# A two-layer encoder on one core: stored-order window projections, 128-row splits, more square buffers and an interleaved last norm

## The chip, the core and the metric

The kernel runs on one core of one Trainium2 chip. TensorE (PE in the profile, with its weight loads as PEld), VectorE (DVE), ScalarE (ACT), GpSimd (POOL) and SyncE (SP), which issues nearly all DMAs, each work through a list of instructions in order and wait for each other through semaphores. The metric is the device time of one execution in microseconds (us). A time is the median of several runs.

## The reference

The kernel computes two layers over 1024 tokens of 1024 features, in fp32, and a last RMSNorm:

```
for l in range(2):
    h = rmsnorm(x, norm_gain[l])
    mk, mv = split(rmsnorm(mem) @ w_mem_kv[l])          # 256 memory tokens
    if l == 0:
        qa, ka, va, qb, kb, vb, qm, gate = split_cols(h @ w_in_even)
        ya = global_gqa(rope_2d(rmsnorm(qa)), rope_2d(rmsnorm(ka)), va)   # 8 heads, 2 kv heads
        yb = window_gqa(qb, kb, vb, sink, rel_bias)                       # 8 heads, +-128 tokens
        ym = memory_attn(qm, mk, mv)                                      # 4 heads of 128
        x = x + (concat(ya, yb, ym) * silu(gate)) @ w_out_even
    else:
        qc, kc, vc, qm, gate = split_cols(h @ w_in_odd)
        yc = neighborhood_attn(qc, kc, vc, rpb)                           # 16 heads, 8x16 window
        ym = memory_attn(qm, mk, mv)
        x = x + (concat(yc, ym) * silu(gate)) @ w_out_odd
return rmsnorm(x, final_norm_gain)
```

## The kernel before

Every fp32 operand of a matmul is held as two parts, a high part rounded for TensorE (`wh`, `ah`, `ph`, the high rows of `q`, `k`, `H`) and a low part, the difference (`wl`, `al`, `pl`). A product is three matmuls: high by high, high by low, low by high. So each weight tile that arrives by DMA (`wraw`) is split: a copy makes the high part, a subtraction the low one. `wsplit` names the engines for the two steps in each stage (lines 131 to 144). Activations lie as features on the 128 rows by tokens on the columns; a projection of 128 features over 1024 tokens is two halves of 24 matmuls of 128x512 (line 223), summed in a PSUM bank `pj`.

The program runs through these stages (times of the profiled execution):

- 0 to 165 us: memory tokens and inputs are loaded and normalised; `mem_keys` (line 489) and `mem_values` (line 518) project the memory for both layers and store keys and values in the DRAM buffer `kv`; the global heads' queries and keys are projected in units of 256 tokens by `a_unit` (line 767), normalised and rotated with the tokens on the rows (`rope`, lines 782 to 801), turned back by TensorE (`back`) and split (`k_unit`, `q_unit`, lines 834 and 849). One half of each tile's rows holds the high part, the other the low part, of one head.
- 165 to 500 us: global attention in pairs of heads (scores in lines 949 and 950, `pv` in line 982).
- 500 to 665 us: window attention in pairs of heads (scores in lines 627 and 628, transposes in line 120, `pv` in line 668). The projections `q_pair`, `k_pair`, `v_pair` for windows are evaluated in natural order of tokens. The tokens are stored in another order: 8 blocks of columns of the 16x64 grid, each with 16 rows of 8. Natural reading makes the moving operand a view of runs of eight floats (`tokens`, `natural=True`). What waits in `self.waiting` (steps of three matmuls of the gate projections, of query projections, of the first output products) is put between the parts of a window pair by `pull`.
- 665 to 790 us: `out_project` of layer 0 (line 1185); the residual sum in line 1194, the squares for the next norm in line 1199 (`square`), their sum on POOL in line 1201.
- 790 to 960 us: `front`, the projections of layer 1; 960 to 1400 us: layer 1's memory and neighbourhood attention.
- 1400 us to the end: `out_project` of layer 1 and the last norm in two halves of 256 tokens each: sums of squares by TensorE (line 264), reciprocal root, turned to rows (line 120), scaled and stored (lines 1619 to 1622).

The order on each engine is made by a scheduler that simulates the program: it moves instructions by priorities (`AHEAD`, `ahead`), by `issue_after` (not before a named matmul has been issued), and keeps the order that is pinned (`Pinned`) on an engine. So the order must be read from the built program.

## Time and profile before

| what | us |
|---|---|
| median of 3 runs (1526.03 to 1527.65) | 1527.34 |
| the profiled execution | 1526.59 |
| its span | 1524.8 |
| TensorE busy (PE) | 1483.9 |
| VectorE busy (DVE) | 1056.7 |
| ScalarE busy (ACT) | 838.3 |
| GpSimd busy (POOL) | 669.4 |
| mean granted clock of TensorE | 0.99 |

A row of a timeline has the start in us, the duration, the engine, the line, the operation, what it writes and reads, and in brackets how long its engine stood idle before it and what released it. A row of the waits has engine, line, releaser, then the sum of the waits, how many, and the longest. A row of a stretch has busy times of the engines, the granted clock (1.00 is full speed), the busy share of the DMA engines and GB/s. A group's row ends with busy time, mean ns of one, and the idle time before them. Times come from one profiled execution; its 1526.59 us lies 0.75 below the median.

### The profile page before, as it was taken

How to read it: one execution, taken by the hardware profiler on the slowest of the kernel's cores; microseconds unless marked ns; L12 is line 12 of the kernel's file. 1: busy time of each engine (PE TensorE's matmuls, PEld its weight loads, DVE VectorE, ACT ScalarE, POOL GpSimd, SP SyncE). 2: the span in 40 equal slices, each digit the busy share in tenths (PEclk: the TensorE clock that was granted, in tenths of full speed). 3: DMA queues.
4: the chain of work that ended last, by engine and by line, in shares of the span. 5: the costliest groups of instructions: out<-in, count | busy, mean ns of one | idle time of the engine just before them, and what ended most of it. 6: DMA issues, size and time to landing. Idle time of an engine off the chain costs nothing.

```text
span 1524.8 us, 25015 instructions
## 1 busy us (share of the span) xinstructions
PE 1483.9 (97%) x8217; PEld 1272.8 (83%) x8217; DVE 1056.7 (69%) x2292; ACT 838.3 (55%) x1854; POOL 669.4 (44%) x793
## 2 busy tenths in 40 slices
PE   8999999999999999999999999999999999999997
PEld 7898898989888788878878777877788888888886
DVE  6688777777676678876577865453477777777754
ACT  7754665555655455655444544453366666666543
POOL 1424546455554545443440000233356566664354
PEclk9999999999999999999999999999999999999998
DMA  8954324233232323287652434575555666678844
GB/s 289 280 166 132 118 70 138 84 101 105 99 99 96 112 67 111 99 287 249 198 183 78 145 116 154 201 243 172 177 167 183 186 205 205 205 218 290 303 120 136
DMA packets 165379, 250.91 MB, mean 165 GB/s; under 512 B 14465, under 2 KB 96641, under 8 KB 164225
## 3 DMA queue, kind: packets, MB, share of 16 engines
q1 hardware_dynamic: 164816, 249.22, 50.6%
q8 instruction: 65, 1.06, 0.3%
q14 instruction: 66, 0.53, 0.1%
q10 hardware_dynamic: 432, 0.09, 0.0%
HBM read 164.32 MB, written 74.45 MB: 157 GB/s over the span
## 4 chain that ended last, share of the span: by engine, by line
PE 85%; DVE 5%; DMA 4%; ACT 2%; issue 2%; POOL 1%; SPq 0%; DVEq 0%; ACTq 0%; POOLq 0%
PE pj L223 28%; PE tr L120 8%; PE pv L982 4%; PE x L1355 4%; PE pj L1185 4%; PE sa L1185 3%; PE pv L1021 3%; PE tr L1185 3%; PE s L1185 2%; PE y L1355 2%; PE pj L373 2%; PE pv L1355 2%; PE sa L949 2%; PE sa L950 2%; PE pv L1185 2%
## 5 line engine op out<-in xcount | busy, mean ns | idle before, releaser
L223 PE MATMUL pj<-H,wh 128*128 128x512 f32 x1280 | 424.9, 412 | 0.6 <-DVE vt L294 0.4
L223 PE MATMUL pj<-H,wl 128*128 128x512 f32 x640 | 252.9, 395 | 0.0
L112 ACT ACTIVATE ph<-tr 128x512 fp32r<-128x512 f32 (+2 forms) x336 | 180.5, 540 | 128.8 <-PE tr L120 123.4
L223 PEld LDWEIGHTS pj<-H,wh 128*128 128x128 f32 x1280 | 220.5, 189 | 33.8 <-PE sa L628 0.8
L470 DVE TENSOR_TENSOR pl<-tr,ph 128x512 fp32r<-128x512 f32 (+2 forms) x336 | 205.0, 615 | 50.6 <-ACT ph L112 48.6
L142 POOL TENSOR_SCALAR wh<-wraw 128x512 fp32r<-128x512 f32 x78 | 50.6, 649 | 279.5 <-DMA g<-P 160.7
L223 PEld LDWEIGHTS pj<-H,wl 128*128 128x128 f32 x640 | 120.4, 188 | 28.6
L112 ACT ACTIVATE wh<-wraw 128x384 fp32r<-128x384 f32 (+1 forms) x162 | 88.1, 552 | 93.5 <-PE pj L1185 11.8
L143 POOL TENSOR_TENSOR wl<-wraw,wh 128x512 fp32r<-128x512 f32 x86 | 113.3, 1318 | 24.7 <-ACT wh L112 20.6
L120 PE MATMUL tr<-ident,P 128*128 128x128 f32 x752 | 116.0, 273 | 2.0 <-POOL P L651 2.0
L1139 POOL TENSOR_TENSOR wl<-wraw,wh 128x384 fp32r<-128x384 f32 x56 | 61.0, 1090 | 107.3 <-ACT wh L112 97.3
L957 POOL TENSOR_SCALAR P<-P,st 128x1024 f32<-128x1024 f32 x64 | 75.7, 1184 | 65.5 <-DVE st L956 65.5
L1052 POOL TENSOR_SCALAR pn<-pn,st 128x384 f32<-128x384 f32 (+1 forms) x128 | 74.9, 588 | 66.8 <-DVE st L1051 37.4
L1050 ACT ACTIVATE pn<-pn,st 128x384 f32<-128x384 f32 (+1 forms) x128 | 75.1, 587 | 41.7 <-DVE st L1049 34.3
L120 PEld LDWEIGHTS tr<-ident,P 128*128 128x128 f32 x752 | 89.1, 140 | 10.5 <-POOL P L651 3.1
L955 ACT ACTIVATE P<-sa,st 128x1024 f32<-128x1024 f32 x64 | 71.6, 1119 | 45.1 <-DVE st L954 25.8
L954 DVE TENSOR_REDUCE st<-sa 128x1 f32<-128x1024 f32 x64 | 77.5, 1217 | 10.4 <-PE sa L950 9.2
L767 PE MATMUL pj<-ah,H 128*128 128x256 f32 x384 | 73.3, 289 | 3.3 <-DVE rqn L793 1.5
L1139 DVE TENSOR_TENSOR wl<-wraw,wh 128x384 fp32r<-128x384 f32 (+1 forms) x64 | 49.4, 771 | 28.5 <-ACT wh L112 28.4
L1046 DVE CUSTOM_DVE_ANT_0 pn<-s,bm 128x384 f32<-128x384 f32 x96 | 53.2, 555 | 19.8 <-PE tr L120 14.7
L982 PE MATMUL pv<-ph,va 128*128 128x256 f32 x256 | 66.6, 285 | 0.0
L982 PE MATMUL pv<-pl,va 128*128 128x256 f32 x256 | 65.8, 284 | 0.0
(488 smaller groups left out, 3919.8 us busy)
## 6 DMA issues: line engine op xcount, KB each, us to landing
wraw<-w_o SPq DMA_DIRECT2D x62, 256.0 KB, 3.5
y<-yb SPq DMA_DIRECT2D x24, 512.0 KB, 3.5
wraw<-s SPq DMA_DIRECT2D x64, 192.0 KB, 3.6
y<-sg SPq DMA_DIRECT2D x23, 512.0 KB, 3.5
wraw<-w_e SPq DMA_DIRECT2D x44, 256.0 KB, 3.0
k<-k SPq DMA_DIRECT2D x40, 256.0 KB, 4.3
wraw<-w_mem SPq DMA_DIRECT2D x32, 256.0 KB, 3.9
v<-v SPq DMA_DIRECT2D x8, 1024.0 KB, 4.8
```

The source lines that it names most:

```text
L112: return self.nc.scalar.activation(out, in_, AF.Copy, scale=scale)
L120: self.turned = self.fence = self.nc.tensor.transpose(o, i, self.ident)
L143: (nc.gpsimd if self.wsplit[1] == "pool" else nc.vector).tensor_tensor(lf, raw, hf, op=OP.subtract)
L223: nc.tensor.matmul(a[:, :n], s[:, kt % UNIT, :], m, start=(kt == 0 and i == 0), stop=(kt == KT - 1 and i == 2))
L470: nc.vector.tensor_tensor(pl[:, :n], tr[:, :n], ph[:, :n], op=OP.subtract)
L954: nc.vector.tensor_reduce(st[:, 0:1], s, axis=AX.X, op=OP.max, negate=True)
L957: self.normal = nc.gpsimd.tensor_scalar(pt, pt, st[:, 2:3], 0.5, op0=OP.mult, op1=OP.mult)
L982: nc.tensor.matmul(o[:, :256], v[:, c + k, kv, :], part[:, k * 256:(k + 1) * 256], start=(c + k == 0 and part is parts[0]), stop=(c + k == ...
L1050: nc.scalar.activation(o, o, AF.Exp, bias=st[:, 1:2], accum_out=st[:, 2:3])
L1139: engine.tensor_tensor(lf, raw, hf, op=OP.subtract)
L1185: last = nc.tensor.matmul(bank, s[:, k, :], y[3 * u + k][m][:, cols], start=start and u + k + e == 0, stop=u == 1 and k + e == 4, skip_gro ...
L1355: self.last = nc.tensor.matmul(bank, ws[s][:, k, :], b[k][m], start=start and k + i == 0, stop=k == UNIT - 1 and i == 2, skip_group_check= ...
```

## The change

Several edits come together:

1. `q_pair` and `k_pair` of the windows project in stored order; the sinks write the result into natural order (`columns`). `v_pair` stays.
2. `mem_values` of layer 0 splits its weights with `wsplit` "both": the low parts take turns on VectorE and POOL.
3. `mem_keys` splits 512 columns at once, `mem_values` uses two tiles of tag "so"; stores for keys are half as many.
4. `back` splits a turned tile on all 128 rows into a high and a low tile. `k_unit` and `q_unit` then place the halves by DMA: for the first query pair into the resident tiles `q0` and the DRAM buffer `qa`, for the second into `qa` alone; for the keys by six DMAs at the end, of which the last two read what they overwrite in the first.
5. `pull(10)` stands ahead of the last window pair.
6. `square` takes its tile from tag "ph" (three buffers in layer 0, four in layer 1) instead of "bt" (one).
7. `finish` replaces the last norm: difference, sum, root, rows and scaling of the two halves are interleaved in a pinned order on VectorE, the turned rows go to two banks, POOL scales three of eight tiles in each half.

```diff
-        (nc.gpsimd if self.wsplit[1] == "pool" else nc.vector).tensor_tensor(lf, raw, hf, op=OP.subtract)
+        e = self.either() if self.wsplit[1] == "both" else nc.gpsimd if self.wsplit[1] == "pool" else nc.vector
+        e.tensor_tensor(lf, raw, hf, op=OP.subtract)
...
+    def columns(self, t, c, n, natural):
+        if not natural:
+            return t[:, c:c + n]
+        return t.rearrange("p (r b c) -> p b r c", b=8, r=16)[:, c // 128:(c + n) // 128]
...
+            if natural:
+                vt = self.st("vt", [128, 512])
+                nc.vector.scalar_tensor_tensor(vt, p, 0.125, self.rows[:, c:c + n], op0=OP.mult, op1=OP.mult)
+                vt = vt.rearrange("p (b r c) -> p b r c", r=16, c=8)
+                self.copy(a[0:64], vt[0:64])
+                self.copy(b[64:128], vt[64:128])
+                nc.vector.tensor_tensor(a[64:128], vt[0:64], a[0:64], op=OP.subtract)
+                nc.vector.tensor_tensor(b[0:64], vt[64:128], b[64:128], op=OP.subtract)
+                return
...
-        self.tokens(w, nt, sink, natural)
+        self.tokens(w, nt, sink)
...
-                    for i in range(2):
-                        hl = [self.st(tag, [128, MEM], F32R) for _ in range(2)]
-                        self.split(*hl, vt[:, i * MEM:(i + 1) * MEM])
-                        for e, t in enumerate(hl):
-                            nc.sync.dma_start(dst[h + i, :, e, :], t.bitcast(F32))
+                    kk = [self.st(tag, [128, 512], F32R) for _ in range(2)]
+                    self.split(*kk, vt)
+                    for e, t in enumerate(kk):
+                        nc.sync.dma_start(dst[h:h + 2, :, e, :].rearrange("h p n -> p h n"),
+                                          t.bitcast(F32).rearrange("p (h n) -> p h n", h=2))
...
-    def back(self, rp, to):
+    def back(self, rp, h, l):
...
+        self.split(h, l, p)
...
+        def end():
+            self.back(rp, *(t[:, c] for t in ks[0]))
             if q == 3:
+                one, two = slice(0, 64), slice(64, 128)
+                for a, b in zip(*ks):
+                    for t, o, f, i in ((b, two, a, two), (b, one, a, two), (a, two, a, one)):
+                        nc.sync.dma_start(t[o].bitcast(F32), f[i].bitcast(F32))
...
+        def end():
+            hl = [self.st("so", [128, 512], F32R) for _ in range(2)]
+            self.back(rp, *hl)
+            for i in range(2):
+                s, o = slice(64 * i, 64 * i + 64), slice(64 - 64 * i, 128 - 64 * i)
+                for to, f in zip((s, o), hl):
+                    f = f[s].bitcast(F32).rearrange("p (t n) -> p t n", t=2)
+                    if pair == 0:
+                        nc.sync.dma_start(q0[i][to, c].bitcast(F32), f[:, 0])
+                        nc.sync.dma_start(qd[1][i, to, c], f[:, 1])
+                    else:
+                        nc.sync.dma_start(qd[0][pair:pair + 2, i, to, c].rearrange("t p n -> p t n"), f)
...
-        self.wsplit = ("act", "pool")
-        end.append(self.mem_values(w0, mem, kvd[0], "mv"))
+        self.wsplit = ("act", "both")
+        end.append(self.mem_values(w0, mem, kvd[0], "so"))
...
-            sq = self.st("bt" if k else "vt", [128, 512])
+            sq = self.st("ph" if k else "vt", [128, 512])
...
+        product(y, p, ws, True, cols[0])
+        difference(p, cols[0])
+        p = self.ps("pj")[:, :256]
+        end = product(y, p, ws, True, cols[1], range(3))
+        with tc.issue_after(end.ins):
+            sum_up(0, sums, True)
+            sum_up(0, [sq], False)
+        with tc.issue_after(self.last.ins):
+            end = product(y, p, ws, True, cols[1], range(3, 6))
+            sum_up(1, sums, True)
...
+                self.pull(10)
             self.window_pair(qb, kb[j // 2], vb, j // 2, 2 * j, sink, y, 1 if j == 2 else 2)
```

GpSimd's (POOL) list in the first stage, from the splits `wl` of the memory values' weights to the splits `al` of the first query weights; `rp` is the sum that ends a rotation. Before:

```order
L143 TENSOR_TENSOR wl_712<-wraw_709,wh_711 128x512
L143 TENSOR_TENSOR wl_724<-wraw_721,wh_723 128x512
L143 TENSOR_TENSOR wl_736<-wraw_733,wh_735 128x512
L143 TENSOR_TENSOR wl_748<-wraw_745,wh_747 128x512
L801 TENSOR_TENSOR rp_929<-rt_182_911,rt_187_925 128x256
L143 TENSOR_TENSOR wl_760<-wraw_757,wh_759 128x512
L753 TENSOR_TENSOR al_808<-wraw_805,ah_807 128x512
```

And now, on the same engine:

```order
L144 TENSOR_TENSOR wl_688<-wraw_685,wh_687 128x512
L144 TENSOR_TENSOR wl_712<-wraw_709,wh_711 128x512
L144 TENSOR_TENSOR wl_736<-wraw_733,wh_735 128x512
L818 TENSOR_TENSOR rp_919<-rt_181_901,rt_186_915 128x256
L144 TENSOR_TENSOR wl_760<-wraw_757,wh_759 128x512
L818 TENSOR_TENSOR rp_943<-rt_188_925,rt_193_939 128x256
L770 TENSOR_TENSOR al_808<-wraw_805,ah_807 128x512
```

Every other `wl` has left this list for VectorE; the first `rp` still stands ahead of the last `wl`.

VectorE's (DVE) list at the end of layer 0: `rows` adds the last square to the sum, `t` are low parts of weights for the next projections, `rq_v` begins the reciprocal root. Before:

```order
L1194 TENSOR_TENSOR yb_8084<-yb_8084,tr_8075 128x512
L1567 TENSOR_TENSOR rows_1675_8071<-vt_8889,bt_9203 128x512
L398 TENSOR_TENSOR t_1974_9362<-wraw_9366,t_1970_9358 128x512
L267 TENSOR_SCALAR rq_v_9316<-pv_9311 128x4
L398 TENSOR_TENSOR t_1975_9363<-wraw_9370,t_1971_9359 128x512
L237 TENSOR_SCALAR rq_i_9318<-rq_v_9316 128x4
L398 TENSOR_TENSOR t_1976_9364<-wraw_9374,t_1972_9360 128x512
L238 TENSOR_SCALAR rq_y_9319<-rq_i_9318 128x4
```

And now:

```order
L1207 TENSOR_TENSOR yb_8026<-yb_8026,tr_8017 128x512
L1656 TENSOR_TENSOR rows_1664_8013<-vt_8831,ph_9145 128x512
L415 TENSOR_TENSOR t_1963_9304<-wraw_9308,t_1959_9300 128x512
L415 TENSOR_TENSOR t_1964_9305<-wraw_9312,t_1960_9301 128x512
L415 TENSOR_TENSOR t_1965_9306<-wraw_9316,t_1961_9302 128x512
L268 TENSOR_SCALAR rq_v_9258<-pv_9253 128x4
L238 TENSOR_SCALAR rq_i_9260<-rq_v_9258 128x4
L239 TENSOR_SCALAR rq_y_9261<-rq_i_9260 128x4
```

The three splits `t` now stand together, ahead of the root.

TensorE's (PE) list at the end of the program; `pj` are the last products, `pv` the sums of squares, the rest turns the roots to rows. Before:

```order
L1185 MATMUL pj_17314<-H_17126,wh_17255 128x256 x2
L1185 MATMUL pj_17314<-H_17126,wl_17256 128x256
L264 MATMUL pv_17283<-inv_d_67,vt_16980 128x1
L264 MATMUL pv_17337<-inv_d_67,vt_16980 128x1 x2
L264 MATMUL pv_17283<-inv_d_67,bt_17259 128x1 x2
L264 MATMUL pv_17337<-inv_d_67,bt_17259 128x1 x2
L120 MATMUL tr_17297<-ident_63,iq_y_17290 128x128 x2
L120 MATMUL tr_17351<-ident_63,iq_y_17344 128x128 x2
```

And now:

```order
L1312 MATMUL pv_17205<-inv_d_67,vt_16922 128x1 x2
L1312 MATMUL pv_17205<-inv_d_67,ph_17204 128x1 x2
L1198 MATMUL pj_17228<-H_17066,wh_17197 128x256 x2
L1198 MATMUL pj_17228<-H_17066,wl_17198 128x256
L1198 MATMUL pj_17228<-H_17067,wh_17197 128x256 x2
L1198 MATMUL pj_17228<-H_17067,wl_17198 128x256
L1198 MATMUL pj_17228<-H_17068,wh_17197 128x256 x2
L1198 MATMUL pj_17228<-H_17068,wl_17198 128x256
L1312 MATMUL pv_17206<-inv_d_67,vt_16922 128x1 x2
L120 MATMUL tr_17264<-ident_63,rq_y_17255 128x128 x2
L120 MATMUL pj_17267<-ident_63,rq_y_17255 128x128 x2
L1312 MATMUL pv_17206<-inv_d_67,ph_17204 128x1 x2
```

The first half's sum has moved in between the second half's products; the second half's sum stands behind the first half's turning.

155 lines of the change are left out of this document (95 added, 60 removed).

## The prediction

> **What bounds the kernel now.** I read the page's busy times first, then stretches of the span, then TensorE's waits, and then the rows around the longest of them.
>
> ```profile
> span 1524.8 us, 25015 instructions
> PE 1483.9 (97%) x8217; PEld 1272.8 (83%) x8217; DVE 1056.7 (69%) x2292; ACT 838.3 (55%) x1854; POOL 669.4 (44%) x793
> ```
>
> TensorE is busy for 1483.9 of 1524.8 us, so only two things can shorten the span: matmuls that take less time, and the 40.9 us in which TensorE does nothing. These waits hold most of the second that the change can reach:
>
> ```profile
> PE pj L518 <- POOL wl L143: 3.1, 3, 1.9
> PE pv L264 <- DVE rows L1567: 2.7, 1, 2.7
> PE pv L668 <- DVE pl L470: 2.6, 2, 1.9
> PE tr L120 <- POOL P L651: 2.0, 4, 0.9
> PE pj L767 <- DVE rqn L793: 1.5, 1, 1.5
> ```
>
> The first is the memory projection at 57 to 61 us, the second the end of layer 0 at 789, the next two the window attention, the last the query units at 114. Stretches (PE, PEld, DVE, ACT, POOL busy; clock; DMA share; GB/s) show what else such a wait costs:
>
> ```profile
> 61.40:64.80 3.40, 3.40 (x14) 2.90 (x14) 3.33 (x5) 2.21 (x5) 2.38 (x2) 0.50 0.91 299
> 112.00:130.00 18.00, 16.24 (x137) 15.84 (x136) 17.57 (x33) 7.48 (x17) 10.38 (x9) 1.00 0.63 193
> 600.00:665.00 65.00, 59.03 (x337) 49.56 (x335) 52.66 (x133) 40.51 (x105) 30.11 (x39) 1.00 0.43 143
> 791.80:798.70 6.90, 6.90 (x22) 5.63 (x23) 4.89 (x17) 3.09 (x6) 0.00 (x0) 0.51 0.73 241
> ```
>
> Behind the first wait the granted clock is 0.50 for 3.4 us, behind the second 0.51 for 6.9 us: a wait there is paid twice. In the window stretch TensorE idles 5.97 us and VectorE is busy 81%; at 112 to 130 us VectorE is busy 98%.
>
> **1. Stored-order reading.** Four query projections and one key projection of the windows, in two halves of 24 matmuls each, no longer gather the tokens in natural order. The chain of waits has such groups of 24:
>
> ```profile
> 412.66 5.50 PE pj L223 x24
> 504.04 5.89 PE pj L223 x24
> 524.26 6.14 PE pj L223 x24
> ```
>
> The first is a stored-order group, the other two natural ones: 0.39 to 0.64 us more. Ten halves give 3.9 to 6.4 us; I take 4.5, since the larger piece holds a little of what follows it. The counts of evictions stay, and only their views become strided:
>
> ```profile
> L678 DVE TENSOR_TENSOR yb<-pv,bt 64x256 f32<-64x256 f32 x32 | 13.2, 414 | 1.4 <-ACT bt L112 1.2
> L988 DVE TENSOR_TENSOR yb<-pv,bt 64x256 f32<-64x256 f32 x32 | 13.2, 412 | 5.6 <-ACT bt L112 5.2
> ```
>
> The windows' sum (L678) writes such strided columns, the global heads' (L988) whole rows, 414 against 412 ns, so I add nothing. Some of these projections fill waits of the window stretch, and a shorter filler there only lengthens a wait: 15% of it lost, **-3.8** (-1 if nearly all of them fill waits, -6.4). The Trainium skill, SBUF — State Buffer, section "Door 1: The DMA port swizzle", says that accesses run at full bandwidth while each 16-byte line is hit at least twice; natural reading takes runs of eight floats, two whole lines, so by that rule it costs nothing and this term would be 0. The rows above speak against it.
>
> **2. The split of the memory values' weights on two engines.**
>
> ```profile
> 59.15 0.73 POOL L801 TENSOR_TENSOR rp<-rt,rt 128x256 f32<-128x256 f32 x1 [1.56 <-DVE rt L798]
> 59.84 1.27 POOL L143 TENSOR_TENSOR wl<-wraw,wh 128x512 fp32r<-128x512 f32 x1
> 61.13 0.33 SPq L124 DMA_DIRECT2D wraw<-w_a  x1
> 61.16 0.62 PE L518 MATMUL pj<-wl,q 128*128 128x512 f32 x1 [1.86 <-POOL wl L143]
> 67.07 0.62 ACT L112 ACTIVATE ah<-wraw 128x512 fp32r<-128x512 f32 x1
> ```
>
> The eighth split stands on POOL behind a rope sum that waits for VectorE. After, four of the eight splits go to VectorE, 0.69 us each; POOL's order still has the sum ahead of the eighth split. The seventh split no longer stands on POOL, and VectorE, on which the sum waited, has no POOL work beside its rope steps; I put both some 1.7 us earlier, near the whole wait of 1.86 (0 if the rope is as late as before). If the halved clock goes too, 3.4 us at half speed return 1.7. What is late next: the last load of w_a is issued only when the eighth split frees its buffer (61.13, behind 59.84+1.27), and its split starts at 67.07, when the first query unit (from 63.1, last quarter some 4.5 us on) needs it. It moves with the split by the same 1.7, so beyond this the gain meets that load. Full price 3.1+1.7 = 4.8; I take **-2.5** (0 if the load decides, -4.8).
>
> **3. Memory keys split once on 512 columns, half the stores.** Fewer, longer operations beside the matmuls of the same projection: 0. The cover is TensorE's own work; without it a longer operation could delay a store by some 0.3 us, and nothing reads these stores before the global heads.
>
> **4. Turned queries and keys split on all rows, halves placed by DMA.**
>
> ```profile
> L849 DVE TENSOR_TENSOR so<-tr,so 64x256 fp32r<-64x256 f32 x24 | 10.1, 423 | 1.5 <-ACT so L112 0.8
> ```
>
> ```profile
> 99.18 4.26 DMA k<-k
> ```
>
> ```profile
> 150.58 0.48 PE L949 MATMUL sa<-k,q 128*128 128x512 f32 x1
> ```
>
> A query unit had four splits of 0.42 us on VectorE; now one of 128x512, 0.69 (as rows, below): 1.0 us less for each of eight units, about 8 us in all, in the stretch where VectorE is the fullest. Of this TensorE can gain no more than its wait of 1.5 at 114. Against it: SyncE issues eight placing DMAs for a unit of the first pair, where there were two, and four for the second pair, where there were also four (two units' worth of tiles): each waits for the split, and weight loads stand behind them. The last two key placings must wait until the first four have read and landed, 4.26 us; the w_a loads queue behind. The first global scores follow only at 150.58, so the placed halves have time. I take **-0.5** (-1.5 the whole wait, +2 half of a second landing for the w_a loads).
>
> **5. Ten gate steps ahead of the last window pair.** The same matmuls, only moved. They are fillers taken from groups whose waits end on VectorE and POOL (2.6 and 2.0 us above); out_project's first products come up to replace them. I take **0** (-3 to +3: half of the 5.97 us either way).
>
> **6. Squares get three buffers (ph) instead of one (bt).** It is a single word of the diff. At the end of layer 0:
>
> ```profile
> 784.54 1.30 POOL L1201 TENSOR_TENSOR vt<-vt,bt 128x512 f32<-128x512 f32 x1 [0.74 <-ACT bt L1199]
> 786.57 1.56 POOL L1201 TENSOR_TENSOR vt<-vt,bt 128x512 f32<-128x512 f32 x1 [0.74 <-ACT bt L1199]
> 786.90 0.67 DVE L1194 TENSOR_TENSOR yb<-yb,tr 128x512 f32<-128x512 f32 x1
> 788.17 0.63 ACT L1199 ACTIVATE bt<-yb 128x512 f32<-128x512 f32 x1 [1.15 <-POOL vt L1201]
> 788.88 1.26 POOL L1201 TENSOR_TENSOR vt<-vt,bt 128x512 f32<-128x512 f32 x1 [0.74 <-ACT bt L1199]
> 790.17 0.63 ACT L1199 ACTIVATE bt<-yb 128x512 f32<-128x512 f32 x1 [1.37 <-POOL vt L1201]
> 790.83 0.69 DVE L1567 TENSOR_TENSOR rows<-vt,bt 128x512 f32<-128x512 f32 x1 [3.25 <-ACT bt L1199]
> 791.67 1.69 PE L264 MATMUL pv<-inv_d,rows 128*128 128x1 f32 x8 [2.71 <-DVE rows L1567]
> 793.39 0.16 DVE L267 TENSOR_SCALAR rq_v<-pv 128x4 f32<-128x4 f32 x1 [0.48 <-PE pv L264]
> 796.53 0.16 DVE L242 SCALAR_TENSOR_TENSOR rq_y<-rq_t,rq_y 128x4 f32<-128x4 f32 x1
> 798.48 0.69 PE L120 MATMUL tr<-ident,rq_y 128*128 128x128 f32 x4
> ```
>
> Each square waits until POOL has added the one before. With three buffers the last square follows its input (ready at 787.57) at 787.6, ends at 788.3; POOL's adds, without the three waits of 0.74, end at 787.9 instead of 790.14; so rows runs from 788.3 to 789.0 instead of ending at 791.52. That is 2.4 of the wait of 2.71. Then the twelve products that fill the rsqrt:
>
> ```profile
> 793.36 5.33 PE x L1355 x12
> 810.69 2.75 PE x L1355 x12
> ```
>
> From 789.1 at the full clock (half of 1.69, then 2.75) they end by 792.8, so the turning of rq_y becomes bound by VectorE. There the order now puts three weight splits (0.69 each) ahead of rq_v: one copy of 0.6 and the three make rq_v start 2.8 us behind rows; the twelve small steps took 3.3 with two splits between them, some 2.4 without; so rq_y is there at 794.2 and the turning starts at 794.3, against 798.48. A new wait of 1.4 us stands in place of 2.71 plus half the clock: **-4.0** (-2.4 if the clock is still halved, -4.7 if VectorE's splits also come earlier). The Trainium skill, TensorE: Matmul & The Clock Gate, Part 1, has the clock halved after an idle window of some 3.4 us, free-running; taken to the letter a wait of 2.71 need not do it, and the term would be the wait alone, -2.4. This trace shows the halving behind 2.71, for two such windows.
>
> **7. The last norm interleaved.**
>
> ```profile
> 1515.54 0.87 DVE L1621 SCALAR_TENSOR_TENSOR H<-H,gain,tr 128x256 f32<-128x256 f32 x2 [0.62 <-ACT vt L112]
> 1518.68 1.65 DVE L1621 SCALAR_TENSOR_TENSOR yb<-yb,gain,tr 128x256 f32<-128x256 f32 x4
> 1520.02 1.44 SPq L1622 DMA_DIRECT2D out<-yb  x2
> ```
>
> VectorE scales twelve tiles in 4.8 us after the last sum; now ten, so 0.8 less, and the first half starts earlier. But half 1's sum stands behind half 0's turning on TensorE, and POOL gets six products instead of four. **-0.7** (-1.3; +0.5 if half 1 comes late).
>
> **Sum.** -3.8 -2.5 -0.5 -4.0 -0.7 = -11.5. The profiled execution took 1526.59 us (span 1524.8 and 1.8 around it), so 1515.1; the median of the runs, 1527.34, lies 0.75 above it: **1515.8, given as 1516**. All lower ends together give 1505, all upper ends 1530.
>
> **Rivals.**
> - *Reading order gains nothing* (by the skill's rule on lines, or because windows wait anyway): the sum without term 1, 1519.6. For it: VectorE at 81% and 5.97 us of waits in that stretch; against it: at 504 to 530 us the groups run back to back. Chance 0.2, taking in other shortfalls of this size.
> - *Prep hands it back*: the w_a load and the clock take terms 2 and 4, and terms 5 and 7 turn: about 1522. Chance 0.15.
> - *Slower: SyncE's queue.* The placing DMAs hold weight loads, in order, behind splits not yet done. For each of the four first units up to six more issues of 0.33 to 0.6 us and one landing of 4.26 could stand ahead of a load: at 4 us a unit TensorE would wait 16 us: 1532. It decides from about 12 us of such waits. Against it: none of the waits quoted at the head is for a transfer. Chance 0.08.
>
> **How the numbers follow.** My forecast, 1508 to 1518.5: 0.57; the rivals as above. A measurement tells about 0.2%, 3.05 us, from no change. Slower than that takes the third rival, 0.08; within it, the upper end of the second, 0.05; faster 0.87. The range reaches from 1508 to 1525: it leaves out the third rival and the tail in which nearly all lower ends meet.
>
> **What would show it.** Term 1: groups of 24 at 5.50 us between 500 and 560 us. Term 2: no wait of pj for wl above 0.7, full clock at 61 to 65. Term 6: rows within 1.5 us of its last input, no clock near 0.5 at 792, and a wait of tr for rq_y of about 1.4. Term 7: last output issued some 0.7 us nearer to the last product. It is wrong if TensorE's waits in the window stretch grow beyond 9 us, or if a weight load ends a wait between 100 and 165 us.

## The result and the profile after

The changed kernel took 1525.1 us (median of 12 runs, 1523.19 to 1532.29), the kernel before in the same series 1526.56 (12 runs, 1522.06 to 1528.31). The ratio is 0.9997, with a 95% interval of 0.9984 to 1.0009: no difference that can be measured. The forecast was a gain of 11.5 us. Of the kernels in the experiments below, one run of a_oldorder took 3755.94 us; it counts in that kernel's median and not in its ratio.

Two lines of the page of after, span and busy times:

```profile
span 1530.5 us, 24962 instructions
PE 1484.7 (97%) x8221; PEld 1273.2 (83%) x8221; DVE 1051.3 (69%) x2263; ACT 828.6 (54%) x1822; POOL 665.1 (43%) x790
```

VectorE and ScalarE have some 5 to 10 us less to do, as the change says, and TensorE has as much as before. This execution took 1532.29, the slowest of its twelve, so both kernels were profiled twice more; the third execution of after (1524.43 us) lies near the median, and most rows below come from it. Its longest waits of TensorE (us in total, times, longest):

```profile
PE s L579 <- ACT k L594: 3.0, 3, 1.9
PE tr L120 <- DVE rq_y L58: 2.8, 2, 2.4
...
PE sa L962 <- DVE q L116: 1.8, 1, 1.8
PE pj L784 <- POOL al L770: 1.8, 1, 1.8
...
PE pj L535 <- POOL wl L144: 1.6, 2, 0.8
PE sa L1198 <- ACT wh L112: 1.5, 1, 1.5
...
PE pv L265 <- DVE rows L1656: 1.1, 1, 1.1
```

The waits that the change was to shorten are shorter: pj for wl 1.6 (3.1 before), pv for rows 1.1 (2.7), pj for rqn gone, and of pv for pl (2.6) there is a tr for pl of 1.7 in three waits. Four stand in their place that before does not have or has shorter: sa for q (the memory's queries, at 147 us), pj for al (60), sa for wh (681), tr for rq_y of the last norm (2.4, at 1512).

Where that leaves the time is read from stretches between the same matmuls of two executions. First the third execution of before, then the third of after: 37 to 160 us (prep), 482 to 722 (window attention) and 722 to 822 (end of layer 0), by the first execution's times; the columns are length, busy time of PE, PEld, DVE, ACT and POOL, clock, DMA share, GB/s.

```profile
35.60:156.90 121.30, 116.12 (x790) 105.32 (x791) 98.33 (x235) 68.91 (x167) 45.23 (x38) 1.00 0.64 198
478.80:719.30 240.50, 234.10 (x1206) 194.19 (x1206) 174.49 (x390) 127.38 (x304) 111.31 (x130) 1.00 0.46 156
719.30:818.90 99.60, 94.79 (x485) 79.78 (x484) 69.60 (x114) 47.19 (x87) 37.64 (x30) 0.98 0.51 166
```

```profile
35.70:158.20 122.50, 116.27 (x790) 105.90 (x791) 87.95 (x208) 60.19 (x136) 39.71 (x34) 1.00 0.71 209
480.20:720.30 240.10, 233.15 (x1205) 194.81 (x1205) 177.88 (x390) 127.24 (x305) 112.27 (x130) 0.99 0.46 154
720.30:818.50 98.20, 95.20 (x484) 79.81 (x483) 68.80 (x115) 47.00 (x87) 37.67 (x30) 0.98 0.55 173
```

All three executions of each, in us, with the halved clock windows of 3.41 us that begin in or reach into the stretch in brackets, where there are any. Lengths are good to some 0.1 us. The last row runs to the end of the span, where the clock is halved in all six:

| stretch (terms) | forecast | before, three executions | after, three executions | middle ones |
|---|---|---|---|---|
| 37-160 (2, 3, 4) | -3.0 | 123.0 (1), 120.9 (0), 121.3 (0) | 123.2 (0), 123.3 (0), 122.5 (0) | +1.9 |
| 160-482 | 0 | 322.0, 322.0, 321.9 | 321.9, 322.0, 322.0 | 0 |
| 482-722 (1, 5) | -3.8 | 240.0 (0), 240.3 (0), 240.5 (0) | 240.4 (1), 240.2 (1), 240.1 (1) | -0.1 |
| 722-822 (6) | -4.0 | 100.0 (2), 100.1 (2), 99.6 (1) | 98.5 (1), 97.8 (1), 98.2 (1) | -1.8 |
| 822-1000 | 0 | 178.0 (1), 178.1 (1), 178.0 (1) | 178.6 (1), 178.1 (1), 177.7 (0) | +0.1 |
| 1000-1045 | 0 | 45.0 (1), 47.9 (2), 45.6 (1) | 51.1 (3), 50.8 (3), 45.5 (1) | +5.2, or 0 |
| 1045-1500 | 0 | 455.0, 456.1, 456.1 | 455.8, 455.0, 455.8 | -0.3 |
| 1500-end (7) | -0.7 | 24.8, 25.1, 24.9 | 25.2, 25.2, 25.2 | +0.3 |

Only the end of layer 0 gained. That gain is firm: of all executions profiled, those of the experiments below included, the sixteen with the squares in ph need 96.9 to 98.7 us for this stretch, the four without 99.6 to 100.1. What it gained, prep lost; the window stretch kept its length; the rest comes and goes between executions of the same kernel. Without the 5 us of the stretch at 1000 (a stall that the third execution of after does not have) the middle ones sum to +0.1.

### The profile page after: what moved, and what is told of

Same layout as the page of the kernel before. It is cut to its first block, busy times and chain, and to the rows that moved or that the text cites. A ratio compares the mean times of both kernels' runs of the same rounds, so it can differ in the third digit from the quotient of the medians.

```text
span 1530.5 us, 24962 instructions
## 1 busy us (share of the span) xinstructions
PE 1484.7 (97%) x8221; PEld 1273.2 (83%) x8221; DVE 1051.3 (69%) x2263; ACT 828.6 (54%) x1822; POOL 665.1 (43%) x790
## 4 chain that ended last, share of the span: by engine, by line
PE 82%; DMA 6%; DVE 5%; ACT 2%; issue 2%; POOL 2%; SPq 0%; POOLq 0%; ACTq 0%; DVEq 0%
PE pj L224 27%; PE tr L120 8%; PE pv L995 4%; PE pj L1198 3%; PE x L1441 3%; PE pv L1034 3%; PE sa L1198 3%; PE pj L784 3%; PE tr L1198 2%; PE s L1198 2%; PE pj L390 2%; PE y L1441 2%; PE pv L1441 2%; PE sa L962 2%; PE sa L963 2%
## 5 line engine op out<-in xcount | busy, mean ns | idle before, releaser
L144 POOL TENSOR_TENSOR wl<-wraw,wh 128x512 fp32r<-128x512 f32 x82 | 106.8, 1304 | 29.9 <-ACT wh L112 25.7
```

What stands on the lines that cost most here:

```text
L144: e.tensor_tensor(lf, raw, hf, op=OP.subtract)
```

## The experiments

All kernels compute everything. Times are medians; the ratio is to the kernel before on the same chip, is taken over the runs, and so need not be the ratio of two medians.

| kernel | us | ratio, 95% |
|---|---|---|
| after_again | 1525.51 | 1.0002 (0.9988-1.0015) |
| a_nopull | 1525.47 | 0.9993 (0.9983-1.0004) |
| a_oldback | 1523.2 | 0.9987 (0.9977-0.9996) |
| a_oldback_2 | 1525.25 | 0.9998 (0.9985-1.0010) |
| a_oldtail | 1524.79 | 1.0006 (0.9989-1.0024) |
| ob_tail | 1525.85 | 1.0009 (0.9995-1.0022) |
| b_order | 1524.97 | 0.9997 (0.9984-1.0010) |
| a_oldorder | 1529.42 | 1.0018 (1.0006-1.0030) |
| b_split_ph | 1525.99 | 0.9994 (0.9979-1.0009) |
| a_poolwh | 1528.29 | 1.0016 (1.0001-1.0031) |
| a_poolwh2 | 1527.01 | 1.0002 (0.9988-1.0016) |
| a_oldkeys | 1529.87 | 1.0022 (1.0008-1.0037) |
| a_oldsplit | 1536.38 | 1.0068 (1.0050-1.0087) |
| best | 1527.11 | 1.0010 (0.9996-1.0024) |
| best_pw | 1525.61 | 1.0003 (0.9990-1.0015) |

### How far one profile can be trusted

Four further executions of the two kernels, unchanged.

> The changed kernel once more. Theory: the profiled execution of 1532.29 us is a single late one; its wait of 4.4 us for ACT k at 1033 us and the halved clock behind it (1036 to 1043) are not in this profile, which shows TensorE level with the kernel before from 960 to 1400 us (about 1.6 us ahead throughout), and a time near 1525. Rival: the wait belongs to the changed kernel and shows again at 1033, with a span near 1530.

> The kernel before, unchanged, for a second profiled execution. Theory: the first one (span 1524.8 us) was lucky between 482 and 722 us, where it has no halved window, and unlucky at 791, where it has two: by stretches between the same matmuls another execution differs from it by up to 2 us, although every instruction is the same, and the differences go with the halved windows. Rival: the stretches repeat to 0.5 us; then what the kernel after loses there is all the change's.

> The kernel before, a third profiled execution: as for the second. Besides: the stall of the next layer at 1033 us, which 3 of the 12 executions of changed kernels show with 2.8 to 4.5 us (the others 0.9 to 2.0), is no part of the change, if one of the executions of before shows it as well; if none does, that stays open.

> The kernel after, a third profiled execution. Theory: the stretches from 722 to 822 us (98.4 and 97.8 against 100.0 of before) and the matmul time from 482 to 722 (231.6 against 233.4) repeat to 0.5 us, the sum of waits and of halved windows does not; the stall at 1033 shows in it or not, with 1.0 or with 2.8 to 4.5 us. Rival: the stall is always there in the kernel after, and the change's.

Measured: spans of 1528.0 (after_again), 1525.8, 1523.5 and 1522.7 us; the stretches stand in the table above. In prep, where no instruction differs, two executions of before are 2.1 and 1.7 us shorter than the first, which had a halved window at 61 us. So the halved clock at 61, with which the prediction's second term started, was that execution's own; the wait for wl ahead of it, 1.85 to 1.86 us, is in all three. At 482 to 722, where the theory put the luck, before has no halved window in any of three executions, after one in each. Before isn't safe from them there either: b_split_ph (below), whose edits lie outside this stretch, has two at 610 us, behind a wait of 2.17 for pl where before waits 1.85, and needs 242.2 us. The stretch at 722 to 822 and the shorter matmuls repeat, as expected.

The stall at 1033 came again in after_again (2.80 us), so it was not one late execution, as that run's theory had it: it is in the first and second execution of after, not in the third, and in none of before (0.8 to 1.1 us there); best, below, shows it with 4.47 us. The rows in the first execution of after:

```profile
1033.31 3.83 DVE L591 TENSOR_SCALAR st<-st 128x2 f32<-128x2 f32 x2
1033.32 3.72 POOL L144 TENSOR_TENSOR wl<-wraw,wh 128x512 fp32r<-128x512 f32 x3
...
1038.24 0.58 PE L579 MATMUL s<-k,q 128*128 128x256 f32 x1 [4.42 <-ACT k L594]
```

Two VectorE steps of 128x2 took 3.83 us beside three GpSimd subtractions that began at the same time. In the third execution of after they began 0.85 us ahead of the subtractions and took 0.90, in the second of before 1.1 us behind them and took 1.39. None of these instructions is touched by the change. That a meeting by tenths of a us decides it fits these rows, but no run tests it, and whether the changed kernel meets more often was not settled.

### Term 1: the stored-order reading

b_order is the kernel before with the new reading alone, a_oldorder the kernel after with the old one:

```diff
-        self.tokens(w, nt, sink, natural)
+        self.tokens(w, nt, sink)
...
+        vt = vt.rearrange("p (b r c) -> p b r c", r=16, c=8)
```

> The kernel before with the stored-order reading alone. Theory: TensorE's matmuls that read the norms for the natural pairs (pj<-H,wh and pj<-H,wl of lines 211 and on) get 3.4 us shorter in sum, as between the profiled before and after (-2.56 and -0.80), and the window pairs hand nearly all of it back, because the scores of a pair now wait for both halves of its queries: a wait of 1.2 to 1.5 us of sa and one of 1.2 to 1.5 us for st near 622, and one halved window of 3.4 us of clock there or later. So the stretch from 482 to 722 us becomes 0.3 to 1.5 us shorter, and the time 0.2 to 1.5 us. Rival, the prediction's first term: the 3.4 to 3.8 us arrive in the time, 1522.5 to 1523. Second rival, its case a: the shorter reading buys nothing because the matmuls were never slowed by it; then no group of matmuls is shorter.

> The kernel after with the natural pairs read and split as before. Theory: the long readings come back (+3.4 us of matmul time between 482 and 722), but the first scores of a window pair wait no more for both halves, and the gate steps still stand ahead of the last pair: the stretch from 482 to 722 is 1 to 3 us longer than in the kernel after, the time 0.5 to 2.5 us longer, 1526 to 1528. Rival: the reading gains nothing in any company, since what it saves is waited for elsewhere; then the time is that of the kernel after to 0.3 us (1525.3).

a_nopull is the kernel after without the line `self.pull(10)`:

> The changed kernel without the ten early gate steps. Theory: the early steps left the last window pair without fillers, so the first products of out_project wait 2.0 us for their weights at 682 to 685 us and the clock is halved for 3.4 us behind them (some 2.2 us); without them both go, and the window stretch keeps about 5 us of small waits: 2 to 4 us faster than the changed kernel, about 1522. Rival: the window stretch is bound by VectorE, the waits only change their place, and the time stays at 1525.

The matmuls did become shorter. The two largest groups of TensorE in 482 to 722, first of before, then of the third execution of after (count | busy us, mean ns):

```profile
L223 PE MATMUL pj<-H,wh 128*128 128x512 f32 x302 | 100.2, 413 | 0.6 <-DVE vt L294 0.4 <-DVE v L353 0.2
L223 PE MATMUL pj<-H,wl 128*128 128x512 f32 x152 | 60.9, 401 | 0.0
```

```profile
L224 PE MATMUL pj<-H,wh 128*128 128x512 f32 x302 | 98.0, 405 | 1.3 <-DVE vt L313 0.9 <-DVE vt L295 0.2
L224 PE MATMUL pj<-H,wl 128*128 128x512 f32 x151 | 59.5, 394 | 0.0
```

That is 3.6 us less; the term had 4.5 before its deduction and 3.8 after. The value pairs keep the natural reading. The stretch keeps its length all the same. In b_order, and alike in a_nopull, the scores of the last pair now wait for both halves of the queries, whose split has become one step behind both:

```profile
620.61 0.69 DVE L316 TENSOR_TENSOR q<-vt,q 64x512 fp32r<-64x512 f32 x1 [0.70 <-ACT q L112]
...
621.35 0.56 PE L643 MATMUL sa<-k,q 128*128 128x256 f32 x2 [1.42 <-DVE q L316]
...
623.56 0.36 PE L643 MATMUL sa<-k,q 128*128 128x256 f32 x1 [1.36 <-DVE st L646]
...
623.90:627.30 3.40, 3.40 (x10) 2.79 (x9) 1.50 (x8) 1.33 (x5) 0.00 (x0) 0.51 0.03 5
```

Two waits of 1.4 us, and the clock at 0.51 for a window behind them: 241.9 us in b_order (which waits another 1.34 at 670), 239.7 in a_nopull, 240.0 to 240.5 in before. With the ten gate steps (after) these waits are gone, and another comes 60 us on:

```profile
679.48 0.63 ACT L112 ACTIVATE q<-q 128x512 fp32r<-128x512 f32 x1 [3.44 <-DMA q<-y]
680.01 0.51 ACT L112 ACTIVATE wh<-wraw 128x384 fp32r<-128x384 f32 x1
...
682.05 0.51 ACT L112 ACTIVATE wh<-wraw 128x384 fp32r<-128x384 f32 x1
...
682.61 0.74 PE L1198 MATMUL sa<-q,wh 128*128 128x512 f32 x2 [1.51 <-ACT wh L112]
...
683.97 0.50 PE L1198 MATMUL sa<-q,wl 128*128 128x512 f32 x1 [0.63 <-DVE wl L1152]
...
684.60:688.00 3.40, 3.40 (x10) 2.62 (x9) 2.98 (x5) 1.68 (x3) 0.96 (x1) 0.50 0.53 188
```

ScalarE holds a weight's high half behind q<-q, which waits 3.44 us for a transfer; TensorE waits 1.51 and 0.63, and the window behind runs at 0.50 of the clock. From the rows of the stretch: PE's busy time is 0.95 less (234.10 to 233.15), to which the half-speed window adds 1.7 by estimate (half of 3.41), and its idle time 0.55 more (6.40 to 6.95). Of the fifteen executions with the new reading, eleven have a halved window in this stretch, of the five with the old one two. In the four without, the stretch is 238.4 (ob_tail), 238.2 (a_oldkeys), 239.2 (a_oldsplit) and 240.9 us (a_oldback_2): three are 1 to 2 us shorter than before, the fourth is not, with more waits (8.8 us in sum, against 6.6 to 7.6). The first rival of b_order, the whole saving in the time, fell, and so did the theory's own range of 0.3 to 1.5 us less in the stretch; the waits and the halved window came as it said. In a_nopull the time is that of after, so its theory of 2 to 4 us fell and its rival held: the waits changed place. In a_oldorder the stretch is 241.6, 1.4 longer than in after, as its theory had it; its time lies 2.5 to 4 us above after's, more than this stretch explains (its prep is 125.1 with a halved window). So within the changed kernel the reading may be worth something that b_order alone does not show. It also has the wait for wh at 689, with 2.66 us: that wait came with the gate steps and not with the reading, while the two at 621 (b_order, a_nopull) came with the reading.

Is ScalarE's queue the cause at 682? a_poolwh copies the first two high halves of the second part's weights on GpSimd, a_poolwh2 all eight:

```diff
-        self.copy(hf, raw)
+        if pool:
+            self.nc.gpsimd.tensor_scalar(hf, raw, 1.0, 1.0, op0=OP.mult, op1=OP.mult)
+        else:
+            self.copy(hf, raw)
...
+                    yield self.w_parts(raw, self.either(), pool=kind == "s1" and not last)
```

> The kernel after; the two high halves of the first weights of the second part of the output projection are copied by GpSimd and not by ScalarE. Theory: TensorE's wait of 1.35 us near 682 us (sa for ACT's wh) is not for the weights, which lay there 5 us before, but for ScalarE's queue, where wh stands behind q<-q, which waits for a transfer. Copied on GpSimd, which is idle for 7 us there, wh is ready by 680, the wait falls to 0.7 or less (q's low halves are due next), and no halved window follows at 685. The stretch from 482 to 722 gets 1.5 to 3 us shorter than in the kernel after (240.2 to 240.4), and of that 1 to 2 us reach the time: 1523 to 1524.5. Rival: it is the transfer of q itself that is late; then the wait goes over to q's halves with the same 1.4 to 1.9 us, the window stays halved, and the time is that of after (1525.3).

> The kernel after; all eight high halves of the second part's weights of the output projection are copied by GpSimd. (The run before it moved the first two, and the wait near 682 stayed at 1.91 us: the two that TensorE waits for are later ones, the copies that ScalarE began at 681.7 and 683.8 us, the first behind q<-q, which waited 3.9 us for its transfer.) Theory: TensorE waits there for ScalarE's queue. With the copies on GpSimd, which is idle from 674 to 682, the wait falls from 1.35 to 1.91 us to 0.6 or less, the one of 0.6 behind it goes too, and no window is halved at 685; the stretch from 482 to 722 is 2 to 3.5 us shorter than in the kernel after (240.2 to 240.4 us), and the time 1 to 2.5 us shorter, 1523 to 1524.5. Rival: what is late are the weights' buffers or their loads; the wait stays over 1 us. Second rival: the wait goes, and the time does not follow, because another wait behind it takes its place.

a_poolwh moved the wrong two: the wait stayed at 1.91, and nothing follows from it (its stretch has two halved windows and 241.9 us). In a_poolwh2 the wait for wh is gone, so ScalarE's queue was what held it, and nothing is won:

```profile
681.56 1.37 DVE L116 TENSOR_TENSOR q<-q 128x512 fp32r<-128x512 f32 x2 [1.85 <-ACT q L112]
682.15 0.62 PE L1201 MATMUL sa<-q,wh 128*128 128x512 f32 x2
...
682.91 1.36 DVE L116 TENSOR_TENSOR k<-k 128x512 fp32r<-128x512 f32 x2
684.19 0.55 DVE L1155 TENSOR_TENSOR wl<-wraw,wh 128x384 fp32r<-128x384 f32 x1
684.80 0.50 PE L1201 MATMUL sa<-q,wl 128*128 128x512 f32 x1 [2.03 <-DVE wl L1155]
```

The low half of the same weight stands on VectorE behind the low halves of q and k, which follow the same late transfer: 2.03 us of wait in place of 1.51 and 0.63, the window at 685.6 halved again, 240.7 us. The second rival held. The same late data hold two queues.

### Terms 2 to 4: prep

b_split_ph is the kernel before with the two engines for the memory values' weights, and with the squares of term 6:

```diff
-        self.wsplit = ("act", "pool")
+        self.wsplit = ("act", "both")
...
-            sq = self.st("bt" if k else "vt", [128, 512])
+            sq = self.st("ph" if k else "vt", [128, 512])
```

> The kernel before with the weights of the memory values split on two engines (parts 2) and the squares of the mixed norm in a buffer of their own (part 6); the two lie 700 us apart, so that each is read at its own place. Theory: the split removes the two waits of pj for wl near 54 and 58 (1.5 to 2.4 us in sum) and the first halved window near 61, and the wait for al behind it takes 0.4 to 1.0 us back: TensorE is 0.5 to 2 us earlier at 76 us, not the 2.5 of the prediction. The squares: rows end about 2 us earlier against what comes before them, the wait for rows falls from over 3 to about 1.0, and the halved window at 792 shrinks from 6.8 to 3.4 us or goes, which makes 1.5 to 2.5 us at 819; about 0.6 goes back at 851 to 856 where x waits for ACT's P. In sum 1.5 to 3.5 us, 1522 to 1524. Rival, the prediction's terms 2 and 6 as they stand: 6.5 us in sum, 1519 to 1520.

In prep it measured 121.2 us without a halved window, as two of the executions of before (120.9, 121.3): the split alone is worth nothing. It cut the wait of pj for wl to 0.86, and TensorE waited 1.27 for another wl at 103 us, and 0.95 and 1.27 for rp at 115 and 121, where before has one wait of 1.5. The squares did what its theory said: 97.5 us from 722 to 822, 2.1 to 2.6 less than before. The time did not follow (0.9994), with two halved windows in the window stretch, as told above.

a_oldback and a_oldback_2 are the kernel after with the turned queries and keys split and placed as before:

```diff
-        self.split(h, l, p)
+        ends = []
+        ...
+        for step in range(2):
+            for e in ends:
+                next(e, None)
```

> The changed kernel with the old splits of turned queries and keys (64 rows, stored from the split). Theory: the wait of 1.8 us ahead of the first global scores at 148 us comes from the full-row split standing ahead of the memory queries on ScalarE and VectorE; with the old splits it goes, a wait of about 1.5 us at 114 us returns, so the same within 1 us. Rival, my forecast's sign: VectorE has 8 us more to do before 150 us and the time is 1 to 2 us longer.

> The kernel after with the old turning of queries and keys, a second time and on another chip perhaps. Its first runs gave 0.9987 of before [0.9977, 0.9996], the same with a mended tail 1.0009 [0.9995, 1.0022]. Theory: the wait of 1.8 us at 148 that it avoids is worth 1 us at most, and the first runs were lucky in their halved windows (mean clock 0.9944 against 0.9924 of the other kernels); it comes out at 0.9990 to 1.0000, 1524.5 to 1526. Rival: it is really 2.3 us faster than before, 0.9987 or less again.

The first gave 0.9987, the second 0.9998, so the 2.3 us of the first were not a gain of this edit. In prep they have 123.0 and 122.8 us, as after; the wait at 147 is gone, and tr waits for rp instead, 0.9 to 1.2 and 1.6 to 1.8 us. So the turning, old or new, is not what prep lost. What makes the wait at 147 in after is order on VectorE and ScalarE:

```profile
147.22 0.60 ACT L112 ACTIVATE so<-tr 128x512 fp32r<-128x512 f32 x1 [4.43 <-PE tr L120]
...
147.72 0.59 ACT L112 ACTIVATE q<-pj 128x512 fp32r<-128x512 f32 x1
...
148.46 0.68 DVE L116 TENSOR_TENSOR q<-pj,q 128x512 fp32r<-128x512 f32 x1
149.20 0.50 PE L962 MATMUL sa<-k,q 128*128 128x512 f32 x1 [1.82 <-DVE q L116]
```

The memory's queries, which the first scores need, are split behind the last unit's turned rows, which wait 4.43 us for their turning.

What prep lost shows between b_split_ph (121.2) and the two a_oldback (123.0 and 122.8), which differ in prep by the new splitting and storing of the memory's keys and values: some 1.7 us. The a_oldback kernels wait 2.02 and 1.59 us near 62 for al, the low half of a query weight, which stands on GpSimd's queue; after waits 1.4 to 1.8. b_split_ph (new weights' split alone) has no such wait, nor have the two kernels below that keep one of the two memory parts and not the other. So it comes where both are together.

The other two parts were then undone one at a time: a_oldkeys has the memory's keys split and stored head by head (`hl = [self.st(tag, [128, MEM], F32R) ...]` in a loop over two heads, as before), a_oldsplit all low halves of the values' weights on GpSimd (`self.wsplit = ("act", "pool")`).

> The kernel after with the memory's keys split and stored head by head as before. What the executions so far say of the stretch from 37 to 160 us, with 1.7 us taken off for each halved window in it: three of the kernel before need 2.1 to 1.7 us less than its first one showed, with the new splitting of the values' weights alone 1.6 less, the kernels with both memory parts new between 0.3 less and 0.5 more (one 1.3 less). Theory: the keys' split on all 512 columns costs 1 to 1.8 us there (TensorE waits 1.8 us for al on GpSimd near 60, which the kernel before does not); without it the wait for al falls under 0.5, and the stretch is 1 to 1.8 us shorter than the kernel after's. Rival: the loss comes from the splitting of the values' weights or from the values' sinks; then the wait for al and the stretch stay (within 0.5 us).

> The kernel after with all low halves of the memory values' weights on GpSimd, as before. The prediction gave the two engines 2.5 us. Theory: they are worth 0.5 or less, because the waits of 1.3 us for wl that they save come back as the one of 1.8 for al; without them wl is waited for with 2 to 3 us again and al with under 0.5, and the stretch from 37 to 160 is within 0.7 us of the kernel after's. Rival, the prediction's term: the stretch is 2 to 3 us longer. The time is that of the kernel after to 1 us in both runs (1524.5 to 1526.5).

The wait for al near 62 is gone in both, but both theories fell on the stretch, and both rivals: prep took 129.6 and 136.3 us, 6 and 13 longer than in after, the times 1.0022 and 1.0068. So undoing the split, which alone is worth nothing, costs 13 us within the changed kernel. TensorE's waits in prep sum to 9.2 and 13.2 us against 6.3 in after; the rest goes with three and five halved windows, where after has none. The waits name a cause that the prediction had as its slower rival. In a_oldsplit SyncE issues 24 placings and stores of turned queries, most of them 0.6 us each, from 108 to 126 us, then stores of the memory's values, and only then the last load of the queries' weights:

```profile
126.79 1.71 SPq L544 DMA_DIRECT2D kv<-so  x3
...
128.59 0.89 SPq L124 DMA_DIRECT2D wraw<-w_a  x1
...
133.03 0.63 ACT L112 ACTIVATE ah<-wraw 128x512 fp32r<-128x512 f32 x1 [5.37 <-DMA wraw<-w_a]
...
133.71 0.80 PE L784 MATMUL pj<-ah,H 128*128 128x256 f32 x4 [3.64 <-ACT ah L112]
```

In a_oldkeys two of these loads stand at 121.5 and 123.1 in the same way, and TensorE waits 4.95 us for ah. In after (third execution) all four were issued at 101.8 to 103.7, ahead of the placings that follow from 106 on. In the two kernels where loads fall behind the placings, prep is 6 to 13 us longer; the kernel after escapes because the planner's order there has them early, and that order changes with either of the two memory parts. What in the planner makes the difference was not pursued.

### Term 7: the last norm

a_oldtail is the kernel after with the last norm as before, so without `finish`. ob_tail is a_oldback with the three GpSimd products of the first half held until the second half's root has run:

```diff
-            self.copy(sb, rows[h][1])
-            for k in range(3):
-                nc.gpsimd.tensor_tensor(at[k][:, c], at[k][:, c], sb, op=OP.mult)
...
+                if k == 6 and not h:
+                    pinned.tensor_copy(sb, rows[h][1])
+                    pool()
```

> The changed kernel with the old last norm in two halves, one after the other. Theory: the interleaved end costs 0.4 us, since the second half's root on VectorE is stretched while POOL scales the first half (steps of 0.65 us in place of 0.16); from the first product of the last tile to the end 16.9 us as before, against 17.3 now: 0.4 us faster than the changed kernel. Rival, my forecast: the old end is 0.7 us longer.

> The kernel after with the old turning of queries and keys (as in the run that gave 1523.2), and with the three products on GpSimd of the last norm's first half held until the second half's root has run on VectorE. Theory: these products stretched VectorE's small steps (rq_t 0.30, rq_t 0.65, rq_y 0.65 us in place of 0.16), so that the second half's row was turned 1.3 us late: without them beside it the three steps take 0.16 us each again, TensorE's wait for rq_y falls from 2.40 to 1.3 to 1.7, and the last store is issued 0.4 to 1.0 us earlier against the last yb difference. Time 1522.2 to 1523.0. Rival: the steps were late for another reason (the queue of VectorE itself, PSUM); then they stay at 0.3 to 0.65 us, and the time is 1523.2 or, by the later products, some tenths more.

The end of after (third execution), then of ob_tail:

```profile
1512.31 2.09 POOL L1334 TENSOR_TENSOR H<-H,vt 128x256 f32<-128x256 f32 x3 [4.23 <-ACT vt L112]
...
1513.08 0.65 DVE L58 SCALAR_TENSOR_TENSOR rq_t<-rq_t,rq_v 128x2 f32<-128x2 f32 x1
...
1513.76 0.65 DVE L58 SCALAR_TENSOR_TENSOR rq_y<-rq_t,rq_y 128x2 f32<-128x2 f32 x1
...
1514.55 0.66 PE L120 MATMUL tr<-ident,rq_y 128*128 128x128 f32 x2 [2.40 <-DVE rq_y L58]
```

```profile
1513.25 0.16 DVE L58 SCALAR_TENSOR_TENSOR rq_t<-rq_t,rq_v 128x2 f32<-128x2 f32 x1
1513.45 0.16 DVE L58 SCALAR_TENSOR_TENSOR rq_y<-rq_t,rq_y 128x2 f32<-128x2 f32 x1
...
1513.76 0.40 PE L120 MATMUL tr<-ident,rq_y 128*128 128x128 f32 x2 [1.30 <-DVE rq_y L58]
...
1514.02 4.15 POOL L1339 TENSOR_TENSOR H<-H,vt 128x256 f32<-128x256 f32 x6 [5.64 <-DVE vt L58]
```

The mechanism is shown: with no GpSimd product beside them the steps take 0.16 us, and TensorE waits 1.30 for the second half's root instead of 2.40. The end did not come earlier: GpSimd now has six products in a row up to 1518.2, and its last tiles are stored last; from 1500 to the end ob_tail and a_oldback both need 25.0 us, and the time was not below a_oldback's. The Trainium skill, SBUF — State Buffer, section "Who interferes with whom", says that a VectorE instruction with two inputs in SBUF contends with a GpSimd instruction that reads SBUF, and that this contention is an exclusive lock; the stretched steps (two inputs, 0.65 for 0.16) agree.

a_oldtail needs 25.4 us there, after 25.2, before 24.8 to 25.1, so neither its theory (0.4 us shorter than after) nor its rival (0.7 longer) shows. Between them the times tell nothing.

### Versions that might beat both

best is the kernel before with the reading, the two engines, the memory's keys and values and the squares as after, and with the old turning, the old last norm and no `self.pull(10)`; best_pw adds the gate steps and the GpSimd copies of a_poolwh.

> The kernel before with the parts of the change that paid at their own places: the stored-order reading, the weights of the memory values on two engines, the mixed norm's squares in their own buffer, the memory keys and values as after; the old turning of queries and keys, the old last norm, and no gate steps ahead of the last pair. Theory, from the stretches: reading -2.0 us of matmul time less the waits of the window pairs (0 to 2), split 0 to -1.5, squares -1.6 to -2.5: 1521.5 to 1524.5, 0.9970 to 0.9990 of before. Rival: what goes at these places is given back at later ones and in halved windows as in every kernel so far, 0.9990 to 1.0005.

> The same with the ten gate steps ahead of the last pair (so that the window pair's scores don't wait) and the two weight halves on GpSimd (so that the output projection doesn't wait for ScalarE's queue). Theory: the two waits of 1.4 us near 621 are gone by the steps, and the one near 682 by GpSimd, each with its halved window: 1 to 2 us less than the run without them, 1520.5 to 1523. Rival: each of the waits only moves; no difference to the run without them.

1.0010 and 1.0003: the rivals held. In best_pw the wait at 686 stays, with 1.66 us, since its GpSimd copies are the wrong two of a_poolwh; that a wait behind the right ones moves is what a_poolwh2 showed. a_oldback, the one kernel whose interval lay below 1, did not repeat. No version here beats the kernel before by more than a measurement can tell.

## Why the prediction was wrong

The forecast was 1516 us, with 1508 to 1525; the median was 1525.1, the profiled execution 1532.29. Of the sum, four terms failed; by the stretches they miss by 4.9 us in prep (terms 2 and 4, with 3), 3.7 in the window stretch, 2.2 at the end of layer 0 and 1.0 in the last norm. That the median lies only just above the range is no merit of the sum: the upper end took in one rival at a time, and here two came true with further losses beside them.

**Term 1 (-3.8).** That the matmuls would shorten was right: 3.6 us less, of 4.5 priced. One of the rows that the price came from, the 24 matmuls of 5.89 at 504, belongs to a projection that keeps its reading (6.09 at 500.7 in the third execution of after), while the group at 489 fell from 6.02 to 5.51. The Trainium skill's rule on 16-byte lines (SBUF — State Buffer, section "Door 1: The DMA port swizzle"), by which the natural reading would cost nothing, does not hold here: 413 against 405 ns as the mean of the wh group, of which only a part was read in the other order. The step that failed is "15% of it lost": in the stretch of after all of it was. The scores came to wait for both halves of the queries, and where the gate steps cover that, ScalarE's and VectorE's queues hold a weight at 682 behind late data; in eleven of fifteen executions a halved window, some 1.7 us by estimate, is added. So what the first rival said came about by the reason it gave second ("windows wait anyway"), not by the rule on lines; its time, 1519.6, did not, since prep handed its gain back as well, as the second rival had it.

**Term 2 (-2.5).** The price was taken from an execution with a halved window at 61 us, which two others do not have. The wait for wl did fall, from 3.1 to 1.6 in sum. The limit named as next (the w_a load and its split, al) came with 1.4 to 1.8 us of wait, and only together with the new keys' split. The step that failed is to count the saved wait as time: alone the split is worth nothing, and within the changed kernel it cannot be priced alone, since without it prep is 13 us longer.

**Term 3 (0) and term 4 (-0.5).** The wait at 114 fell from 1.5 to 1.0, as far as expected. What was not seen is the wait of 1.8 at 147, for the memory's queries behind the last unit's rows, now split as one piece; it cancels term 4's gain, since prep is as long with the old turning. Term 3 was put at nothing because its operations stand beside TensorE's own work; together with term 2 it brought the wait for al, and prep some 1.7 us. With term 2 they make +1.9 where -3.0 was forecast. Why the keys' split, before the first query unit, makes al late was not traced further. The third rival, SyncE's queue, did not happen in after and did in a_oldsplit and a_oldkeys, with its own mechanism: weight loads behind the placings, TensorE waiting 3.64 and 4.95 us in one piece. The range of term 4 (-1.5 to +2) ended too low for that.

**Term 5 (0).** Right in the sum (a_nopull 239.7 against 240.1 to 240.4, each with one halved window), by changing one wait for another.

**Term 6 (-4.0).** Half right: -1.8 over the stretch. From the third execution of after, at the end of layer 0:

```profile
781.12 6.43 POOL L1214 TENSOR_TENSOR vt<-vt,ph 128x512 f32<-128x512 f32 x4 [3.02 <-ACT ph L1212]
...
784.85 1.54 DVE L58 TENSOR_TENSOR wl<-wraw,wh 128x512 fp32r<-128x512 f32 x1 [0.17 <-ACT wh L112]
786.32 0.68 DVE L1207 TENSOR_TENSOR yb<-yb,tr 128x512 f32<-128x512 f32 x1
...
787.82 0.69 DVE L1656 TENSOR_TENSOR rows<-vt,ph 128x512 f32<-128x512 f32 x1 [0.83 <-ACT ph L1212]
788.66 1.02 PE L265 MATMUL pv<-inv_d,rows 128*128 128x1 f32 x8 [1.08 <-DVE rows L1656]
...
790.40:793.80 3.40, 3.40 (x10) 2.63 (x9) 2.88 (x15) 0.21 (x1) 0.00 (x0) 0.50 0.94 301
```

The square follows its input at once and rows follows the square, as the term had it. But the input comes later: GpSimd's four sums now run without a pause, and the weight split beside them takes 1.54 us, where the third execution of before has

```profile
784.77 0.68 DVE L58 TENSOR_TENSOR wl<-wraw,wh 128x512 fp32r<-128x512 f32 x1
```

In before such subtractions take 1.31 and 1.43 us where they begin beside a running sum (783.53, 781.38), and this one began in a pause. That this is the hold seen in the last norm is argued from the rows, not shown by a run. The wait of 1.08 with the eight one-column sums still halves one window. That turned out to cost little: where it is not halved (a_nopull, 98.0 us) TensorE waits 1.08 for rq_y, about the wait of 1.4 that the term foresaw, so VectorE sets the end either way. Another 0.9 us was lost between the turning and 819. The term was mis-sized: -1.8 for -4.0, and rows end 1.6 us earlier against the matmuls before them, not 2.5. Part of the miss is the price: against the products ahead of it the turning comes 3.1 us earlier than in the execution that the term was priced from, which has two halved windows there, but 1.4 earlier than in before's third, which has one.

**Term 7 (-0.7).** +0.3. The step "half 1's sum stands behind half 0's turning" was seen; that GpSimd's products of half 0 stretch the root of half 1 was not.

**The signs.** Several of the signs that the prediction named came true, and the time did not: in after the clock is full at 61 to 65, the waits for wl are 0.82 and 0.75 (the sign said 0.7), rows end 1.5 us after their last input, no weight load ends a wait between 100 and 165, and TensorE's waits in the window stretch stay under 9 us. The clock near 0.5 at 792 did not go. Each sign looked at the place that was priced; what was lost lay beside it.

## What to carry to other kernels

A part that shortens filler work in a stretch with many waits is worth what the waits leave of it, so ask which data the next wait is for, and whether several queues hold for the same data. Before a wait of one profile is priced, see whether it and the halved clock behind it are there in a second and third execution. Where a planner sets the order, parts that share a queue are one change: price them together, and look at the order of the loads in the shared queue first.

## What the runs showed of the hardware

**The spread of one kernel goes with its halved windows.** Over 105 runs of the kernel before, three series of 35 (1519.61 to 1530.01 us), the nine with a mean granted clock of 0.990 or less have a median of 1529.06, the twelve with 0.995 or more 1522.45. One halved window takes 0.0011 off the mean clock (half of 3.41 us in 1523). In the trace's clock record halved windows of one execution begin whole multiples of 3.413 us apart (684.58, 790.393 and 1008.846 in the third execution of after: 31 and 64 of them), so whether the same wait halves the clock depends on where it falls in this grid. The Trainium skill, TensorE: Matmul & The Clock Gate, Part 1, has this free-running window, and the half clock after one idle window of about 3.4 us; here less idleness was enough. The window ahead of 684.58 holds waits of 1.4 and 0.6 us and 1.3 us of matmuls. In ob_tail the same two waits (1.52 and 0.61 us) fall into two windows of its grid, and none is halved.

**Some 1.8 us of idleness in one window halve the next.** If all 20 traces are divided by their own grids (20 to 1500 us, one-column matmuls counted as idle), 77 of the 78 windows at full clock ahead of a halved one hold 1.74 us or more without a matmul (the last 1.44); of the 8522 others eight do, and none more than 1.89. So a wait of 1.85 us, as the one for wl ahead of 61, is at the edge: it lies whole in one window in the first and second execution of before, and halved the clock in the first; in the third it falls into two windows.

**VectorE beside GpSimd.** VectorE's smallest steps, 0.16 us alone, took 0.3 to 0.65 us beside back-to-back products on GpSimd, and two of them 3.83 at 1033; a 128x512 subtraction took 1.54 for 0.68. An edit that lets GpSimd run without pauses can lengthen what VectorE does beside it: ob_tail shows it for term 7, for term 6 it is argued.
